# Sums of squares and a norm on TensorE, and two partial transforms in one PSUM bank, in a diffusion step's filter stage

## The chip, the cores and the metric

The kernel runs on one core of a Trainium2 chip. The metric is the time of one execution on the device, in microseconds (us). The engines are named as in the profile: TensorE is PE (its weight loads are PEld), VectorE is DVE, ScalarE is ACT, GpSimd is POOL, and SyncE (SP) issues DMAs.

## The reference

One inference step of a two-layer network on 1024 latent and 128 context tokens of width 1024: a layer of differential attention, then a Hyena layer with a long convolution, each followed by a SwiGLU layer. What the change touches is the first norm (`rmsnorm` ahead of the queries, keys and values) and the implicit filter of the convolution with its spectrum:

```python
def rmsnorm(x, g, eps=EPS):
    xf = x.astype(jnp.float32)
    y = xf * lax.rsqrt(jnp.mean(xf * xf, axis=-1, keepdims=True) + eps)
    return (y * g.astype(jnp.float32)).astype(x.dtype)

def implicit_filter(L, w1, b1, w2, b2, w3, b3, freq):
    ...
    h = (hdn @ w3.astype(f32) + b3.astype(f32)).reshape(L, 2, D_MODEL)
    ...
    h = h * jnp.exp(-t[:, None, None] * deltas)
    return h / (jnp.sum(jnp.abs(h), axis=(0, 1), keepdims=True) + FILT_EPS)

def bidir_fftconv(v, filt):
    ...
    kk = jnp.concatenate([h_f, jnp.zeros((1, D), filt.dtype), h_b[:0:-1]], axis=0)
    vf = jnp.fft.rfft(v.astype(jnp.float32), n=n, axis=1)
    kf = jnp.fft.rfft(kk, n=n, axis=0)
    return jnp.fft.irfft(vf * kf[None], n=n, axis=1)[:, :L]
```

## The kernel before

All data is float32, and large products are made of three TensorE matmuls on a high and a low part of each operand (`three`: high by high, low by high, high by low). A scheduler that simulates a timeline sets the order of each engine's instructions outside the stretches that the program pins; it takes buffers from pools as they come free. The pools that matter here: five PSUM banks `mm`, three PSUM banks `aux`, three buffers each of `wh`, `wl` and `bf`, two of `nsq`.

The first stage, `filters`, makes the filter and its spectrum for eight channel tiles of 128 channels, and beside it works off a generator, `start`, seven steps for each tile. `start` loads x, computes modulation vectors (`ada_step`, 32 small matmuls and a transpose each), and for each of three chunks of 384 tokens computes the row norm and the modulated input of the projection. Its norm: for each of eight row tiles, ScalarE squares x into `nsq`, GpSimd adds it into `nacc` (`square`, L445 and L449); then three one-column matmuls with a vector of ones sum `nacc` over partitions (L464), VectorE finishes the reciprocal root, and three matmuls with a diagonal (L484) broadcast it. Each of eight products and modulations follows (L553 to L557).

For a channel tile, `filter_time` computes the filter in time with 27 matmuls into five `mm` banks, VectorE multiplies by the decay into `filt` (L1425). ScalarE takes absolute values of the two combinations, VectorE their maximum (`am`), then sums it over eight blocks with stride 128 (L1442) and TensorE sums over partitions (L1447) for the norm `den`. GpSimd patches row 0 (L1453 to L1456). `hilo` splits each of two parts into high and low (L1432, L1433).

`filter_spectrum` transforms one part in four residues j = 0 to 3 of time modulo 4 (`dft`, six matmuls each). Residues 0 and 2 fill the two halves of one bank, 3 and 1 a bank each:

```python
        X3, X1 = self.mm(), self.mm()
        self.dft(X3, zh, zl, slice(0, 512), 3)
        self.dft(X1, zh, zl, slice(0, 512), 1)
        ...
        tt(f[:, 2], X1[:, part], s[:, part], ADD)
        tt(f[:, 3], X1[:, 1 - part], s[:, 1 - part], SUB)
```

ScalarE copies residue 3 to SBUF, VectorE makes the sum and difference (these butterflies have the line of the helper `tt`, L1288), GpSimd the last four, and a DMA stores them. Behind the stage come the projections `qk` (24 matmuls of 384 columns into each bank), which start with chunks 0 and 1 while chunk 2 is still being modulated.

## Time and profile before

| | |
|---|---|
| median of three runs | 3115.69 us (3109.5 to 3119.96) |
| the profiled execution | 3119.61 us, its span 3117.8 us |
| TensorE busy in the span | 3028.1 us (97%), weight loads 2957.7 us |
| VectorE, ScalarE, GpSimd busy | 1959.6, 1170.3, 964.1 us |
| mean granted TensorE clock | 0.990 of 2.4 GHz |

The span runs from the first instruction to the last; the rest of the execution's time, 1.8 us, lies outside it. Times of stretches are counted from the span's start. A matmul's record covers its way through the array, so records overlap, and a float32 matmul that is not split into parts leaves two records.

### The profile page before, as it was taken

The numbers are of one execution on the slowest core, as the hardware profiler recorded it, in microseconds if no ns is written. First come the engines' busy times: TensorE is split into PE (matmuls) and PEld (weight loads), VectorE is DVE, ScalarE is ACT, GpSimd is POOL, SyncE is SP. The second block draws the span as 40 slices with busy tenths as digits, with TensorE's granted clock in tenths as the row PEclk, the third lists the DMA queues.
The fourth block names the chain that finished last, engine by engine and source line by source line (L and its number), as shares of the span: only waits on it lengthen the run. The fifth ranks groups of instructions, "written<-read, shape, count | busy, mean of one in ns | idle before, by whom it ended". The sixth has DMA issues, their size and how long they took to land.

```text
span 3117.8 us, 52555 instructions
## 1 busy us (share of the span) xinstructions
PE 3028.1 (97%) x20963; PEld 2957.7 (95%) x20963; DVE 1959.6 (63%) x3223; ACT 1170.3 (38%) x2242; POOL 964.1 (31%) x842
## 2 busy tenths in 40 slices
PE   6889999999999999999999999999999999999998
PEld 5679999999999999999999999999999999999998
DVE  7866532888845745454568878876456444445555
ACT  3631123888835322223211442334644222222114
POOL 5844310444432334342000423221223343430003
PEclk9999999999999999999999999999999999999999
DMA  7665462334241222223555433345621222225211
GB/s 251 200 209 189 136 171 89 78 87 102 63 148 59 75 78 72 78 72 124 217 206 179 141 111 112 135 152 183 212 74 64 75 75 75 75 78 202 99 64 68
DMA packets 164635, 380.13 MB, mean 122 GB/s; under 512 B 17407, under 2 KB 80263, under 8 KB 161576
## 3 DMA queue, kind: packets, MB, share of 16 engines
q1 hardware_dynamic: 149016, 354.42, 34.6%
q10 hardware_dynamic: 13968, 17.65, 1.6%
q0 software_dynamic: 1408, 4.72, 0.4%
q8 instruction: 165, 2.70, 0.4%
q14 instruction: 78, 0.64, 0.1%
HBM read 279.99 MB, written 96.73 MB: 121 GB/s over the span
## 4 chain that ended last, share of the span: by engine, by line
PE 82%; DVE 5%; DMA 3%; issue 1%; POOL 1%; ACT 1%; SPq 0%; POOLq 0%; ACTq 0%; DVEq 0%
PE mm L308 12%; PE mm L310 12%; PE mm L309 12%; PE pr L310 11%; PE pr L308 11%; PE pr L309 10%; PE tr L820 4%; PE sc L794 2%; PE tr L811 2%; PE sc L795 2%; DMA araw<-ada_w 1%; DVE junk L402 1%; DVE xk L892 1%; DMA zt<-d_z 1%; DVE wl L1674 1%
## 5 line engine op out<-in xcount | busy, mean ns | idle before, releaser
L310 PE MATMUL mm<-hs,wl 128*128 128x384 f32 x1632 | 547.0, 336 | 0.0
L309 PE MATMUL mm<-hs,wh 128*128 128x384 f32 x1632 | 546.5, 335 | 0.4 <-POOL hs L498 0.3
L308 PE MATMUL mm<-hs,wh 128*128 128x384 f32 x1632 | 545.4, 336 | 0.9 <-DVE xk L892 0.9
L1288 DVE TENSOR_TENSOR xk<-pr,xk 128x576 f32<-128x576 f32 x202 | 152.5, 755 | 389.9 <-PE pr L310 203.9
L892 DVE SCALAR_TENSOR_TENSOR xk<-mm,ada,xk 128x192 f32<-128x192 f32 (+3 forms) x560 | 232.5, 453 | 255.4 <-PE mm L310 249.7
L449 POOL TENSOR_TENSOR nacc<-nacc,nsq 128x384 f32<-128x384 f32 x104 | 123.2, 1186 | 661.3 <-ACT nsq L445 659.3
L308 PEld LDWEIGHTS mm<-hs,wh 128*128 128x128 f32 x1632 | 306.2, 188 | 4.1 <-PE mm L310 1.5
L1673 ACT ACTIVATE wh<-raw 128x1024 fp32r<-128x1024 f32 x156 | 164.9, 1058 | 384.9 <-PE mm L309 333.8
L310 PEld LDWEIGHTS mm<-hs,wl 128*128 128x128 f32 x1632 | 306.4, 188 | 3.0 <-issue 1.6
L309 PEld LDWEIGHTS mm<-hs,wh 128*128 128x128 f32 x1632 | 306.4, 188 | 2.7 <-issue 0.6
L1288 POOL TENSOR_TENSOR xk<-xk,xk 128x576 f32<-128x576 f32 x80 | 116.8, 1461 | 524.9 <-DVE xk L1288 430.7
L1674 DVE TENSOR_TENSOR wl<-raw,wh 128x1024 fp32r<-128x1024 f32 x156 | 196.9, 1262 | 67.1 <-ACT wh L1673 66.7
L1674 DVE TENSOR_TENSOR wl<-xk,wh 128x512 fp32r<-128x512 f32 x160 | 174.1, 1128 | 48.3 <-ACT wh L1673 48.3
L308 PE MATMUL mm<-hh,wh 128*128 128x384 f32 x576 | 193.5, 339 | 2.4 <-ACT hh L556 1.8
L801 DVE TENSOR_REDUCE nm<-sc 128x1 f32<-128x1152 f32 x128 | 173.6, 1357 | 34.9 <-PE sc L795 34.8
L309 PE MATMUL mm<-hl,wh 128*128 128x384 f32 x576 | 194.6, 338 | 0.8 <-DVE hl L557 0.8
L310 PE MATMUL mm<-hh,wl 128*128 128x384 f32 x576 | 194.4, 338 | 0.0
L803 ACT ACTIVATE pr<-sc,nm 128x1152 f32<-128x1152 f32 x128 | 156.7, 1224 | 14.7 <-DVE nm L801 8.9
L1077 ACT ACTIVATE xk<-xk 128x576 f32<-128x576 f32 x40 | 27.4, 686 | 352.2 <-DVE xk L1288 352.2
L794 PE MATMUL sc<-kk,qs 128*128 128x384 f32 x384 | 140.5, 366 | 3.3 <-ACT pr L803 3.3
L820 PE MATMUL tr<-v,at 128*128 128x128 f32 x1152 | 139.4, 275 | 0.5 <-ACT at L815 0.5
L820 PEld LDWEIGHTS tr<-v,at 128*128 128x128 f32 x1152 | 133.8, 192 | 3.1 <-ACT at L815 0.9
(388 smaller groups left out, 8794.5 us busy)
## 6 DMA issues: line engine op xcount, KB each, us to landing
raw<-w_gu SPq DMA_DIRECT2D x88, 512.0 KB, 3.3
d_a<-xk SPq DMA_DIRECT2D x82, 288.0 KB
raw<-w_down SPq DMA_DIRECT2D x44, 512.0 KB, 4.2
araw<-d_a SPq DMA_DIRECT2D x36, 576.0 KB, 6.5
araw<-ada_w SPq DMA_DIRECT2D x36, 512.0 KB, 6.0
kk<-d_k SPq DMA_DIRECT2D x16, 1152.0 KB, 8.7
araw<-ada_t SPq DMA_DIRECT2D x28, 512.0 KB
raw<-w_in SPq DMA_DIRECT2D x24, 512.0 KB, 4.0
```

The costliest lines, as they stand in the source:

```text
L308: self.nc.tensor.matmul(out, ah, bh, start=first, stop=False, **kw)
L309: self.nc.tensor.matmul(out, ah, bl, start=False, stop=False, **kw)
L310: self.nc.tensor.matmul(out, al, bh, start=False, stop=last, **kw)
L449: nc.gpsimd.tensor_tensor(out=self.acc[c], in0=self.acc[c], in1=sq, op=ALU.add)
L794: nc.tensor.matmul(sc[:, c, :CH], lhs, kk[:, 0, p, ks], start=True, stop=False)
L801: nc.vector.tensor_reduce(out=nm, in_=sv, axis=AX.XY, op=ALU.max, negate=True)
L803: nc.scalar.activation(e.rearrange("p (a b) -> p a b", a=3), sv, AF.Exp, bias=nm, accum_out=st[hd][3][:, p, qt : qt + 1])
L820: self.nc.tensor.matmul(po[:, :P], at[:, b], v[:, b], start=b == 0, stop=b == 8)
L892: self.nc.vector.scalar_tensor_tensor(out=x, in0=ps[:, s:e], scalar=gate[:, d, g : g + 1], in1=x, op0=ALU.mult, op1=ALU.add)
L1288: (eng or self.nc.vector).tensor_tensor(out=o, in0=a, in1=b, op=op)
L1673: self.nc.scalar.activation(hi, x, AF.Copy)
L1674: (eng or self.nc.vector).tensor_tensor(out=lo, in0=x, in1=hi.bitcast(F32), op=ALU.subtract)
```

## The change

It does three things in the filter stage. The squares of `start` are no longer added by GpSimd: each is the stationary operand of three one-column matmuls with ones, which accumulate over the eight row tiles in one `aux` bank, and `rstd_parts` starts from that bank. The filter norm's sum over eight blocks is likewise done by eight accumulating one-column matmuls instead of VectorE's strided sum. And residues 1 and 3 accumulate in one bank: a second transform table (`k_filt`) holds residue 3 with the sine half negated, and for the second part the high and low parts of residue 3 are negated in `hilo`, so that the bank holds the sum in one half and the difference in the other.

```diff
--- before.py
+++ after.py
@@ -80,6 +80,9 @@
     ph = 2 * math.pi * ((2 * k[None, :] + 1) * tm[:, None] % 4096) / 4096
     fm = np.concatenate([np.cos(ph), -np.sin(ph)], axis=1)
     out["k_fwd"] = fm.reshape(2, P, 4, 512).transpose(1, 2, 0, 3).reshape(P, 8 * 512)
+    sign = np.ones((4, 512))
+    sign[3, 256:] = -1.0
+    out["k_filt"] = (fm.reshape(2, P, 4, 512) * sign).transpose(1, 2, 0, 3).reshape(P, 8 * 512)
     gm = fm.T / 1024.0
     out["k_inv"] = gm.reshape(4, P, 256, 4).transpose(1, 3, 0, 2).reshape(P, 16 * 256)
     k = np.arange(128)
@@ -458,8 +461,8 @@
 
     def rstd_parts(self, c, early=False):
         nc, acc = self.nc, self.acc[c] if isinstance(self.acc[c], tuple) else [self.acc[c]]
-        ps = self.aux()
-        for t in range(3):
+        ps = self.acc[c] if early else self.aux()
+        for t in range(0 if early else 3):
             for n, a in enumerate(acc):
                 nc.tensor.matmul(
                     ps[:, t : t + 1], a[:, P * t : P * t + P], self.ones[:, 0:1], start=n == 0, stop=n == len(acc) - 1
@@ -542,8 +545,19 @@
             return t
 
         for c in range(NCH):
+            self.acc[c] = self.aux()
             for k in range(KT):
-                self.square(c, k, source(c, k))
+                sq = self.tl(self.np_, [P, CH], tag="nsq", bufs=2)
+                nc.scalar.activation(sq, source(c, k), AF.Square)
+                for t in range(3):
+                    nc.tensor.matmul(
+                        self.acc[c][:, t : t + 1],
+                        sq[:, P * t : P * t + P],
+                        self.ones[:, 0:1],
+                        start=k == 0 and t == 0,
+                        stop=k == KT - 1,
+                        skip_group_check=True,
+                    )
                 yield
             rs = self.rstd(c, True)
             hh, hl = self.hpair()
@@ -1296,8 +1310,8 @@
             self.split(hi[:, o : o + step], lo[:, o : o + step], raw)
         return hi, lo
 
-    def forward_table(self, pool, raw_pool, raw_tag):
-        t = self.table(pool, self.i["k_fwd"], 4096, "t", raw_pool, raw_tag, 2048, 2 if raw_tag == "filt" else 1)
+    def forward_table(self, pool, raw_pool, raw_tag, src="k_fwd"):
+        t = self.table(pool, self.i[src], 4096, "t", raw_pool, raw_tag, 2048, 2 if raw_tag == "filt" else 1)
         self.fwd = [t.rearrange("p (j m f) -> p j m f", j=4, m=2) for t in t]
 
     def sine(self, halves, vec, j):
@@ -1360,7 +1374,7 @@
             c = slice(H * q, H * q + H)
             nc.scalar.activation(hids[0][:, c], hid[:, c], AF.Copy)
             nc.vector.tensor_tensor(out=hids[1][:, c], in0=hid[:, c], in1=hids[0][:, c].bitcast(F32), op=ALU.subtract)
-        self.forward_table(sp, sp, "filt")
+        self.forward_table(sp, sp, "filt", "k_filt")
         self.d_w = [self.tl(self.dp, [P, 2, P], F32, f"d_w{c}") for c in range(KT)]
         with self.tc.issue_after(mark.ins):
             w = [self.filter_weights(0), self.filter_weights(1)]
@@ -1387,10 +1401,10 @@
         for _ in rest:
             pass
 
-    def dft(self, out, zh, zl, cols, j):
+    def dft(self, out, zh, zl, cols, j, first=True, last=True):
         for m in range(2):
             a, f = 2 * j + m, [t[:, j, m, cols] for t in self.fwd]
-            self.three(out, zh[:, a], zl[:, a], *f, first=m == 0, last=m == 1)
+            self.three(out, zh[:, a], zl[:, a], *f, first=first and m == 0, last=last and m == 1)
 
     def filter_weights(self, ct):
         nc, i, sp, tt = self.nc, self.i, self.sp, self.tt
@@ -1423,14 +1437,21 @@
                 self.three(out, hid[0][:, t], hid[1][:, t], wh, wl)
             d = dec[:, a0 : a0 + m] if m == 2 else decp.unsqueeze(1)
             tt(filt[:, a0 : a0 + m], ps[:, : 256 * m].rearrange("p (a f c) -> p a f c", a=m, f=2), d.unsqueeze(2).to_broadcast([P, m, 2, P]), MUL)
-        sm = self.tl(sp, [P, 2, P], tag="fsum", bufs=1)
+        sm = self.tl(sp, [P, P], tag="fsum", bufs=1)
         self.zs = []
 
         def hilo(part):
             zh = self.tl(self.wp, [P, 8, P], F32R, tag="wh", bufs=3)
             zl = self.tl(self.wp, [P, 8, P], F32R, tag="wl", bufs=3)
-            nc.scalar.activation(zh, filt[:, 0:8, part], AF.Copy)
-            tt(zl, filt[:, 0:8, part], zh.bitcast(F32), SUB)
+            for a, b, sign in ((0, 6, 1.0), (6, 8, -1.0)) if part else ((0, 8, 1.0),):
+                z = filt[:, a:b, part]
+                nc.scalar.activation(zh[:, a:b], z, AF.Copy, scale=sign)
+                if sign > 0:
+                    tt(zl[:, a:b], z, zh[:, a:b].bitcast(F32), SUB)
+                else:
+                    nc.vector.scalar_tensor_tensor(
+                        out=zl[:, a:b], in0=z, scalar=sign, in1=zh[:, a:b].bitcast(F32), op0=MUL, op1=SUB
+                    )
             self.zs.append((zh, zl))
 
         am = self.tl(self.wp, [P, 8, P], tag="wh", bufs=3)
@@ -1439,12 +1460,12 @@
         nc.scalar.activation(am2, filt[:, 0:8, 1], AF.Abs)
         yield
         tt(am, am, am2, ALU.max)
-        nc.vector.tensor_reduce(out=sm[:, 0], in_=am.rearrange("p a c -> p c a"), axis=AX.X, op=ADD)
         nc.scalar.activation(am2[:, 0:2], filt[:, 8], AF.Abs)
-        tt(sm[:, 1], am2[:, 0], am2[:, 1], ALU.max)
+        tt(sm, am2[:, 0], am2[:, 1], ALU.max)
         ps = self.aux()
-        for g in range(2):
-            nc.tensor.matmul(ps[:, g : g + 1], sm[:, g], self.ones[:, 0:1], start=True, stop=True)
+        for a in range(8):
+            nc.tensor.matmul(ps[:, 0:1], am[:, a], self.ones[:, 0:1], start=a == 0, stop=a == 7)
+        nc.tensor.matmul(ps[:, 1:2], sm, self.ones[:, 0:1], start=True, stop=True)
         den = self.den[:, ct]
         nc.vector.tensor_scalar(out=den, in0=ps[:, 0:2], scalar1=FILT_EPS, scalar2=None, op0=ADD)
         nc.vector.reciprocal(den, den)
@@ -1468,22 +1489,19 @@
         X = self.mm()
         self.dft(X[:, 0:256], zh, zl, main, 0)
         self.dft(X[:, 256:512], zh, zl, main, 2)
-        s = self.tl(sp, [P, 2, 256], tag="xs", bufs=3)
-        nc.scalar.activation(s[:, 0], X[:, 256:512], AF.Copy)
-        tt(f[:, 0], X[:, 0:256], s[:, 0], ADD)
-        tt(f[:, 1], X[:, 0:256], s[:, 0], SUB)
-        X3, X1 = self.mm(), self.mm()
-        self.dft(X3, zh, zl, slice(0, 512), 3)
-        self.dft(X1, zh, zl, slice(0, 512), 1)
-        s = self.tl(sp, [P, 2, 256], tag="xs", bufs=3)
-        nc.scalar.activation(s, X3.rearrange("p (a b) -> p a b", a=2), AF.Copy)
-        X1 = X1.rearrange("p (a b) -> p a b", a=2)
-        tt(f[:, 2], X1[:, part], s[:, part], ADD)
-        tt(f[:, 3], X1[:, 1 - part], s[:, 1 - part], SUB)
-        tt(K[:, 0], f[:, 0], f[:, 2], ADD, nc.gpsimd)
-        tt(K[:, 2], f[:, 0], f[:, 2], SUB, nc.gpsimd)
-        tt(K[:, 1], f[:, 1], f[:, 3], SUB if part else ADD, nc.gpsimd)
-        tt(K[:, 3], f[:, 1], f[:, 3], ADD if part else SUB, nc.gpsimd)
+        s = self.tl(sp, [P, 256], tag="xs", bufs=3)
+        nc.scalar.activation(s, X[:, 256:512], AF.Copy)
+        tt(f[:, 0], X[:, 0:256], s, ADD)
+        tt(f[:, 1], X[:, 0:256], s, SUB)
+        Y = self.mm()
+        self.dft(Y, zh, zl, slice(0, 512), 1, last=False)
+        self.dft(Y, zh, zl, slice(0, 512), 3, first=False)
+        nc.scalar.activation(f[:, 2:4], Y.rearrange("p (a b) -> p a b", a=2), AF.Copy)
+        s, d = f[:, 2 + part], f[:, 3 - part]
+        tt(K[:, 0], f[:, 0], s, ADD, nc.gpsimd)
+        tt(K[:, 2], f[:, 0], s, SUB, nc.gpsimd)
+        tt(K[:, 1], f[:, 1], d, SUB if part else ADD, nc.gpsimd)
+        tt(K[:, 3], f[:, 1], d, ADD if part else SUB, nc.gpsimd)
         nc.scalar.dma_start(self.d_f[ct][:, part], K)
 
     def hyena_in(self, first):
```

What the scheduler made of it, in three places. The first is VectorE where the first channel tile's filter is finished, ahead of the first transform; `wh` and `wl` hold the maximum and the high and low parts, `th` and `tl` the table. Before:

```order
L1288 TENSOR_TENSOR filt_347<-mm_380,ndg_319 128x256
L1288 TENSOR_TENSOR wh_386<-wh_386,wl_387 128x1024
L1442 TENSOR_REDUCE fsum_385<-wh_386 128x128
L1288 TENSOR_TENSOR fsum_385<-wl_387 128x128
L1288 TENSOR_TENSOR wl_404<-filt_347,wh_403 128x1024
L1288 TENSOR_TENSOR wl_408<-filt_347,wh_407 128x1024
L1449 TENSOR_SCALAR den_218<-aux_394 128x2
L514 TENSOR_TENSOR tl_300<-filt_305,th_299 128x2048
```

Now:

```order
L1302 TENSOR_TENSOR filt_347<-mm_380,ndg_319 128x256
L1302 TENSOR_TENSOR wh_386<-wh_386,wl_387 128x1024
L1302 TENSOR_TENSOR fsum_385<-wl_387 128x128
L1302 TENSOR_TENSOR wl_410<-filt_347,wh_409 128x1024
L1302 TENSOR_TENSOR wl_414<-filt_347,wh_413 128x768
L1452 SCALAR_TENSOR_TENSOR wl_414<-filt_347,wh_413 128x256
L1470 TENSOR_SCALAR den_218<-aux_393 128x2
L1471 RECIPROCAL den_218<-den_218 128x2
L517 TENSOR_TENSOR tl_300<-filt_305,th_299 128x2048
```

The strided sum is gone, the second low part is two instructions, and what follows stands as it was.

The second is TensorE at the first row norm, between the filter products (`wsh`, `wsl`) of the third channel tile. Before and now:

```order
L382 MATMUL aux_582<-ident_203,ndg_580 128x128
L1447 MATMUL aux_697<-ones_207,fsum_646 128x1 x2
L464 MATMUL aux_771<-ones_207,nacc_587 128x1 x3
L309 MATMUL mm_834<-wsl_603,hidh_293 128x256
L310 MATMUL mm_834<-wsh_602,hidl_294 128x256
```

```order
L385 MATMUL aux_590<-ident_203,ndg_588 128x128
L553 MATMUL aux_595<-ones_207,nsq_596 128x1 x3
L553 MATMUL aux_595<-ones_207,nsq_601 128x1 x3
L1467 MATMUL aux_708<-ones_207,wh_663 128x1 x8
L1468 MATMUL aux_708<-ones_207,fsum_662 128x1
L553 MATMUL aux_595<-ones_207,nsq_606 128x1 x3
L311 MATMUL mm_884<-th_299,wh_724 128x256
```

In place of three sums of the finished `nacc` and two of the norm stand groups of three, one group for each square, and nine for the norm; of the chunk's eight groups three stand here and five between the transforms that follow.

The third is TensorE where the projection begins (`hh`, `hl` are its inputs, `aux` from `ndg` the broadcast of the third chunk's norm). Before, with the projection's products around it, and now, with those of the transform of the last tile but one:

```order
L309 MATMUL mm_2272<-hl_795,wh_2256 128x384
L310 MATMUL mm_2272<-hh_794,wl_2257 128x384
L308 MATMUL mm_2272<-hh_794,wh_2256 128x384
L309 MATMUL mm_2272<-hl_795,wh_2256 128x384
L484 MATMUL aux_1939<-ndg_1940,ones_207 128x128
L484 MATMUL aux_1939<-ndg_1943,ones_207 128x128
L1447 MATMUL aux_2075<-ones_207,fsum_2024 128x1 x2
L310 MATMUL mm_2272<-hh_794,wl_2257 128x384
L308 MATMUL mm_2272<-hh_794,wh_2256 128x384
```

```order
L313 MATMUL mm_2142<-th_299,wl_1961 128x256
L311 MATMUL mm_2142<-th_299,wh_1960 128x256
L487 MATMUL aux_1989<-ndg_1990,ones_207 128x128
L487 MATMUL aux_1989<-ndg_1993,ones_207 128x128
L1467 MATMUL aux_2120<-ones_207,wh_2075 128x1 x8
L1468 MATMUL aux_2120<-ones_207,fsum_2074 128x1
L312 MATMUL mm_2142<-tl_300,wh_1960 128x256
L313 MATMUL mm_2142<-th_299,wl_1961 128x256
L311 MATMUL mm_2159<-th_299,wh_1960 128x512
```

The broadcast and the last norm now stand ahead of the last transforms instead of inside the projection; the first projection product comes some 65 rows behind them. Past TensorE's row 1041 of 18124 the instructions are in the same order on all engines as before, apart from line and buffer numbers.

## Rows read from the trace of the kernel before

**Rows 1.** The page's slices: tenths busy of 40 slices of 78 us.
```profile
PE   6889999999999999999999999999999999999998
...
DVE  7866532888845745454568878876456444445555
```

**Rows 2.** Busy time by stretch: columns, the stage, three parts of it.
```profile
core 0: us, PE busy (x) PEld busy (x) DVE busy (x) ACT busy (x) POOL busy (x), PEclk, DMA share, GB/s
37.00:185.00 148.00, 128.40 (x1131) 108.48 (x1130) 128.68 (x202) 78.90 (x142) 106.75 (x123) 0.93 0.54 184
...
82.00:112.00 30.00, 23.32 (x234) 19.20 (x234) 25.46 (x38) 19.65 (x38) 25.96 (x32) 0.94 0.72 251
...
142.00:166.00 24.00, 20.43 (x188) 17.39 (x189) 21.22 (x31) 12.06 (x23) 14.95 (x18) 0.86 0.65 230
...
166.00:185.00 19.00, 19.00 (x118) 15.92 (x118) 15.24 (x28) 11.10 (x18) 10.84 (x12) 0.98 0.32 118
```

**Rows 3.** The waits of TensorE, 37 to 185 us: in total, times, longest.
```profile
PE mm L308 <- DVE filt L1288: 8.8, 3, 3.6
...
PE mm L310 <- DVE wl L1288: 3.2, 2, 2.9
...
PE mm L308 <- DVE bf L1288: 1.5, 1, 1.5
```

**Rows 4.** Groups by form, 37 to 185 us: busy and mean ns, idle before.
```profile
L449 POOL TENSOR_TENSOR nacc<-nacc,nsq 128x384 f32<-128x384 f32 x20 | 23.4, 1169 | 9.4 <-ACT nsq L445 8.9
...
L1288 DVE TENSOR_TENSOR bf<-mm,xs 128x256 f32<-128x256 f32 x60 | 22.1, 410 | 7.0 <-ACT xs L1479 3.1 <-PE mm L310 1.5 <-POOL nsq L1288 1.4
...
L1288 DVE TENSOR_TENSOR filt<-mm,raw 128x512 f32<-128x512 f32 x28 | 17.9, 678 | 0.4 <-PE mm L310 0.2
...
L1442 DVE TENSOR_REDUCE fsum<-wh 128x128 f32<-128x1024 f32 x8 | 16.3, 2039 | 0.1
```

**Rows 5.** The chain of waits, 172.5 to 175 us: start, us, what.
```profile
172.69 0.23 PE mm L310
...
173.04 0.34 PE aux L1447 x4
...
173.38 0.67 PE aux L464 x6
```

**Rows 6.** VectorE's timeline at the stage's start: start, us, operation, count, idle before.
```profile
35.33 2.00 DVE L1442 TENSOR_REDUCE fsum<-wh 128x128 f32<-128x1024 f32 x1
...
38.59 3.59 DVE L1288 TENSOR_TENSOR wl<-filt,wh 128x1024 fp32r<-128x1024 f32 x2 [0.64 <-ACT wh L1432]
```

**Rows 7.** TensorE's waits at the projection's start, 185 to 235 us.
```profile
PE aux L371 <- DMA araw<-ada_w: 2.0, 3, 1.3
...
PE mm L308 <- ACT hh L556: 1.8, 3, 1.0
...
PE mm L309 <- DVE hl L557: 0.8, 1, 0.8
```

**Rows 8.** Further waits, 37 to 185 us.
```profile
DVE wh L1288 <- ACT wl L1439: 6.6, 3, 3.8
...
POOL nsq L1288 <- DVE filt L1288: 4.1, 1, 4.1
...
ACT nsq L445 <- POOL nacc L449: 2.1, 4, 1.0
```

**Rows 9.** VectorE's timeline at three places.
```profile
81.60 3.79 DVE L553 TENSOR_TENSOR hl<-aux,hl 128x384 f32<-128x384 f32 x8
...
101.35 8.64 DVE L1288 TENSOR_TENSOR wl<-filt,wh 128x1024 fp32r<-128x1024 f32 x2 [0.68 <-ACT wh L1432]
...
161.59 1.21 DVE L1288 TENSOR_TENSOR wl<-filt,wh 128x1024 fp32r<-128x1024 f32 x1
```

**Rows 10.** TensorE's timeline behind two such blocks.
```profile
86.05 0.50 PE L308 MATMUL mm<-th,wh 128*128 128x512 f32 x1 [2.52 <-DVE filt L1288]
...
142.91 0.58 PE L308 MATMUL mm<-th,wh 128*128 128x256 f32 x1 [3.63 <-DVE filt L1288]
```

## The prediction

> **What bounds the kernel now.** The page's slices come first [rows 1]: TensorE is at nine tenths or more in all but the first few of 40 slices, each 78 us long. The reader should see that only slices 0 to 2 leave TensorE room, and that VectorE is fuller there than almost anywhere else. That is the filter stage, and every instruction the change touches lies in it or just behind it. The second view is busy time in that stage [rows 2]: from 37 us, where the first norm sum runs, to 185 us, where the query and key projection starts, VectorE works 128.7 of 148.0 us. TensorE's matmul records cover 128.4, its weight loads 108.5, GpSimd 106.8. So no engine is full, and VectorE is the tightest. TensorE's granted clock there is 0.93: (1 − 0.93) × 2 × 148 = 20.7 us at the lower of its two levels, 1.2 instead of 2.4 GHz, which costs half of that, 10.4 us. It is low where TensorE waits, 0.94 from 82 to 112 and 0.86 from 142 to 166 us, and 0.98 from there to 185, where its records leave no gap.
>
> The third view is who ended TensorE's waits [rows 3]: VectorE's filter products 8.8 us, its low parts 3.2, its butterflies 1.5, together 13.5. So in this stage TensorE runs behind VectorE, which is what the change unloads; but it loads TensorE.
>
> **Part by part.** All sums are against the profiled execution (span 3117.8, own time 3119.6 us); the median of the three runs, 3115.7, lies 3.9 lower.
>
> *Two partial transforms in one bank.* The matmul count stays: the four products of index 3 and index 1 go into one bank instead of two. VectorE loses two of four butterflies per part, 32 in all, at 410 ns [rows 4]: 13.1 us. ScalarE copies 512 columns as before, now into the result. The sign costs no instruction in part 0 (it is in the table, whose load has the same size) and splits the high and low part in part 1: eight more instructions on each of VectorE and ScalarE. VectorE's operations on 512 and 256 columns at 678 and 410 ns [rows 4] leave a fixed part of 0.142 us, so 1.1 us in eight; ScalarE works 78.9 of 148 us [rows 2] and hides its own.
>
> *The filter norm.* VectorE's eight strided sums of 2.04 us go, 16.3 us [rows 4]. TensorE gets nine one-column matmuls per channel tile instead of two: 56 more.
>
> *The sums of squares.* GpSimd's 21 additions go; 20 of them lie in the stage, 23.4 us [rows 4]. TensorE gets 72 one-column matmuls instead of 9: 63 more.
>
> *What the 119 cost.* Each float32 matmul appears as two records: in the chain, six records are three row-norm matmuls, 0.67 us, 0.112 us a record, and four records at the norm take 0.34 us [rows 5]. A 512-column matmul beside them takes 0.23, so a column count of one buys only half of it. 119 × 2 × 0.112 = **+26.6 us** of TensorE.
>
> Does TensorE have that room? By matmul records it is idle 19.6 of 148 us [rows 2], too little; by weight loads 39.5, enough. The added work is weight loads with almost nothing to stream, and I go by the loads. The Trainium skill ("Perfetto Trace Analysis", Identifying the Most-Contended Engine) says that matmul busy share is a poor measure of TensorE's headroom, since matmuls are pipelined, and to use that of weight loads. By it the added work fits; by the matmul records the stage would come out 7 us longer at least.
>
> *What TensorE gets back.* VectorE falls from 128.7 to 128.7 − 13.1 − 16.3 + 1.1 = 100.4 us, so the 13.5 us of waits for it can go: **−13.5** (0 to −13.5; the larger end, since 28 us is twice the wait). With TensorE denser the lower clock goes too: **−10.4** (0 to −10.4; the larger end, because it is 0.98 from 166 us, where TensorE does not wait).
>
> *The start of the stage.* In VectorE's timeline the first strided sum, 2.00 us, stands ahead of the low parts [rows 6], for which the first transform waits. It goes: **−2.0** (0, if ScalarE's copy, which already ends a wait of 0.64 there, is late; no more than 2.0).
>
> *The start of the projection.* As the order shows, the third token chunk's norm is broadcast before the last two transforms instead of inside the projection, so that chunk should be ready earlier. TensorE waits there 1.8 for its high parts and 0.8 for its low parts [rows 7]: **−2.6** (0 to −2.6). The waits for weights from DMA, 2.0, stay: SP's queue keeps its loads and only shifts the chunk's loads among them.
>
> *New waits.* A square's buffer, one of two, is freed by TensorE instead of GpSimd, and the row that patches the filter uses the same two; an auxiliary bank of three is held from a chunk's first square to its norm. Behind a late buffer stand ScalarE's next square and GpSimd's patch, and behind that the high parts and the transform. ScalarE waited 2.1 us for GpSimd there before, and GpSimd's patch 4.1 for VectorE [rows 8]. I take 0, the old wait for the new one; the ends are −2.1 and +4.1.
>
> Sum: 26.6 − 13.5 − 10.4 − 2.0 − 2.6 = **−1.9 us**: 3117.7 as profiled, 3113.8 on the scale of the median. Past the first projection tiles the instructions stand in the same order as before, so what the stage gains or loses is kept. A measurement of this kernel can tell about 0.3%, 9.3 us, from no change; this is within it.
>
> **Rivals.** *Faster.* The added loads fall into idle time that remains. Of the 39.5 us in which no weights load, 13.5 + 10.4 are used above; if the other 15.6 take part of the 26.6, only 11.0 lie on the path and the sum is −17.5 (3098.2 on the median's scale). For it: most added matmuls come in groups of three as each square is ready, scattered through the stage. VectorE may gain more than counted: two low-part operations took 8.64 us where GpSimd worked beside them, one took 1.21 us late in the stage, where GpSimd stood idle [rows 9]. The Trainium skill ("GPSIMD Engine Reference", Specifications) says that GpSimd and VectorE contend for SBUF when VectorE has two SBUF inputs; by that, less GpSimd work makes VectorE faster still, and the trace agrees (8.64 against 1.21). Against it: TensorE runs its queue in order, and a group waiting for a square holds up transforms behind it.
>
> *Slower.* TensorE becomes the bound while the waits stay. Two of the longest, 2.52 and 3.63 us, come behind blocks of eight norm products on VectorE, 3.79 us each, which the change does not touch [rows 9, 10]. If only the rest, 7.4, goes, and the clock stays low behind those two (0.94 over 30 us and 0.86 over 24 us, 1.8 + 3.4 lost [rows 2]), 5.2 comes back there and nothing at the two starts: 26.6 − 7.4 − 5.2 = +14.0, so 3129.7. It decides from where TensorE gets back less than 26.6 − 9.3 = 17.3 us of the 28.5 counted. Against it: VectorE has 28 us less ahead of these blocks.
>
> *The change does little to VectorE*, because its waits only move: VectorE ends as early but waits for ScalarE's absolute values (6.6 us before [rows 8]). Then the gains shrink by half, 26.6 − 14.2 = +12.4, so 3128.1; it counts with the slower case.
>
> **How the numbers follow.** No change 0.51, around 3113.8, on its own 3106 to 3125; faster 0.29, around 3098; slower 0.20, around 3129. The faster case gets more because one unknown, the overlap of scattered loads, works for it alone. The range, 3098 to 3127, takes in the faster case's middle and half of the slower one and leaves some 0.2 outside.
>
> **What would show it.** In the profile after: one-column matmuls at some 0.11 us a record, and TensorE's weight loads near 135 us in the stage; VectorE near 100 us; TensorE's waits for VectorE under 4 us; a granted clock over 0.97 between 64 and 166 us; the projection's first matmul within 5 us of 184. Wrong would be: the records far cheaper than 0.11 us; waits of TensorE for squares or for banks of some microseconds in all; a clock as low as before; or a time that moves without the stage moving.

## The result, and the profile after

The changed kernel takes 3135.55 us (median of 4, 3132.96 to 3136.44) where the kernel before, on the same chip, takes 3112.65 (4 runs): a ratio of 1.0064, 95% interval 1.0051 to 1.0077, some 20 us slower. That lies above the range given. The profiled execution after took 3135.16 us, its span 3133.4; the one before, at 3119.6, was 7 us slower than its median, so the two spans differ by 15.6 us and the medians by 22.9.

Busy time by stretch of the kernel after (PEclk is the granted clock), against [rows 2]:

```profile
core 0: us, PE busy (x) PEld busy (x) DVE busy (x) ACT busy (x) POOL busy (x), PEclk, DMA share, GB/s
37.00:185.00 148.00, 146.26 (x1228) 131.67 (x1229) 79.55 (x149) 73.34 (x136) 75.60 (x92) 0.83 0.49 168
...
166.00:185.00 19.00, 19.00 (x106) 16.66 (x101) 5.38 (x8) 5.77 (x10) 4.50 (x7) 0.50 0.43 131
...
37.00:211.30 174.30, 172.56 (x1370) 155.55 (x1371) 94.51 (x179) 84.74 (x158) 86.74 (x104) 0.82 0.46 157
```

All of TensorE's waits from 37 to 211 us (total, times, longest), against [rows 3]; then those of the projection's start, 211 to 262 us, against [rows 7]:

```profile
PE mm L311 <- ACT wh L1448: 0.9, 1, 0.9
PE mm L311 <- DVE filt L1302: 0.8, 1, 0.8
...
PE mm L311 <- ACT hh L570: 1.5, 1, 1.5
PE mm L312 <- DVE hl L571: 0.5, 1, 0.5
```

TensorE's timeline after: start, us, operation, count.

```profile
98.54 0.40 PE L312 MATMUL mm<-tl,wh 128*128 128x512 f32 x1
98.77 0.61 PE L487 MATMUL aux<-ndg,ones 128*128 128x128 f32 x4
99.22 1.84 PE L1467 MATMUL aux<-ones,wh 128*128 128x1 f32 x16
100.92 0.25 PE L1468 MATMUL aux<-ones,fsum 128*128 128x1 f32 x1
...
161.05 1.84 PE L1467 MATMUL aux<-ones,wh 128*128 128x1 f32 x16
162.75 0.36 PE L1468 MATMUL aux<-ones,fsum 128*128 128x1 f32 x2
162.98 1.48 PE L553 MATMUL aux<-ones,nsq 128*128 128x1 f32 x12
164.38 1.90 PE L374 MATMUL aux<-hl,cs 128*32 128x128 f32 x30
...
171.55 0.63 PE L311 MATMUL mm<-th,wh 128*128 128x512 f32 x1
171.98 0.63 PE L312 MATMUL mm<-tl,wh 128*128 128x512 f32 x1
...
185.98 3.41 PE L1467 MATMUL aux<-ones,wh 128*128 128x1 f32 x16
189.25 0.57 PE L1468 MATMUL aux<-ones,fsum 128*128 128x1 f32 x2
...
211.29 0.34 PE L311 MATMUL mm<-hh,wh 128*128 128x384 f32 x1
```

The reader should see three things. TensorE's waits, 13.5 us for VectorE alone before, are down to 1.7 in all: its records cover 146.26 of 148 us. VectorE fell from 128.7 to 79.6 us. And the clock, which was to rise, fell from 0.93 to 0.83, to 0.50 all the way from 166 to 185 us, where no record of TensorE leaves a gap. That drop begins behind 30 one-column records in a row (161.05 to 164.38), where the small matmuls of a modulation vector follow (L374). What it costs is in the same rows: 16 one-column records last 1.70 us at full clock (99.22 to 100.92) and 3.27 at the lower one (185.98 to 189.25), a transform's 512 columns 0.23 and 0.43. The projection starts at 211.3 us instead of 184.1.

So the time up to the projection splits as follows. The clock loses (1 − 0.82) × 174.3 = 31.4 us where it lost (1 − 0.93) × 147.1 = 10.3: **+21.1**. TensorE's idle time by records falls from 147.1 − 127.5 = 19.6 to 174.3 − 172.6 = 1.7: **−17.9**. The start moves by +27.2, so the added work comes to 27.2 − 21.1 + 17.9 = **+24.0**, near the 26.6 forecast. Behind the start 11.6 us comes back between the two profiles (27.2 against 15.6 in the spans), or 4.3 against the medians (22.9).

The column of the clock has a blind spot at the start: ahead of a trace's first clock record it reads 1.00. A product of 256 columns at 46 us, first in the kernel before, then after:

```profile
46.15 0.28 PE L310 MATMUL mm<-th,wl 128*128 128x256 f32 x1
```

```profile
46.08 0.41 PE L312 MATMUL mm<-tl,wh 128*128 128x256 f32 x1
```

TensorE came to its full clock (its warm-up) at 43.8 us before and at 48.4 after, by the first clock records; 0.93 and 0.83 count the time from 37 us to there as full. These 4.6 us more at the lower level cost 2.3, which belong to the clock and leave some 22 for the added work.

### The profile page after: what moved, and what is told of

It reads as the page before. It is cut to its first block, busy times and chain, and to the rows that moved or that the text cites. A ratio compares the mean times of both kernels' runs of the same rounds, so it can differ in the third digit from the quotient of the medians.

```text
span 3133.4 us, 52972 instructions
## 1 busy us (share of the span) xinstructions
PE 3067.5 (98%) x21201; PEld 3004.6 (96%) x21201; DVE 1919.4 (61%) x3191; ACT 1172.8 (37%) x2250; POOL 940.6 (30%) x821
## 4 chain that ended last, share of the span: by engine, by line
PE 88%; DMA 5%; DVE 3%; ACT 2%; issue 1%; POOL 1%; SPq 0%; ACTq 0%; POOLq 0%; DVEq 0%
PE mm L311 14%; PE mm L312 14%; PE mm L313 14%; PE pr L313 10%; PE pr L311 10%; PE pr L312 10%; PE tr L834 4%; PE sc L808 2%; PE sc L809 2%; PE tr L825 2%; DMA araw<-ada_w 1%; ACT xk L943 1%; PE aux L553 1%; PE tr L311 1%; PE tr L313 1%
## 5 line engine op out<-in xcount | busy, mean ns | idle before, releaser
L452 POOL TENSOR_TENSOR nacc<-nacc,nsq 128x384 f32<-128x384 f32 x83 | 98.2, 1184 | 649.3 <-ACT nsq L448 647.6
## 6 DMA issues: line engine op xcount, KB each, us to landing
kk<-d_k SPq DMA_DIRECT2D x16, 1152.0 KB, 11.6
```

Source lines behind the costliest of these rows:

```text
L452: nc.gpsimd.tensor_tensor(out=self.acc[c], in0=self.acc[c], in1=sq, op=ALU.add)
```

## The experiments

Two theories, in the words of the expectations. A: the one-column matmuls bring TensorE to its lower clock. B: any 26 us of added TensorE work costs this much on an engine that has become full. C, in the first runs: the new order of instructions is at fault. "Lower clock" is the time at the lower level from warm-up to the projection's first matmul, 2 × (1 − PEclk) × duration of that stretch, taken from the trace's clock records, which are finer than the two digits of the rows; each stretch's row stands with its run.

### The parts of the change alone

**The bank part alone** (`bank_only`): the change with its squares and its norm undone.

```diff
-                for t in range(3):
-                    nc.tensor.matmul(self.acc[c][:, t : t + 1], sq[:, P * t : P * t + P], self.ones[:, 0:1], ...)
+                self.square(c, k, source(c, k))
...
-        for a in range(8):
-            nc.tensor.matmul(ps[:, 0:1], am[:, a], self.ones[:, 0:1], start=a == 0, stop=a == 7)
+        nc.vector.tensor_reduce(out=sm[:, 0], in_=am.rearrange("p a c -> p c a"), axis=AX.X, op=ADD)
```

> Of the change only the two transforms in one bank; squares are added by GpSimd and the norm by VectorE's strided sum again. Theory A (the one-column matmuls bring TensorE's clock down): none are added, so the low clock stays at some 20 us or less in the stage, VectorE has 12 us less, and the time is 0 to 8 us below before. Theory B (any 26 us of added TensorE work costs this much): no work is added, also 0 to 8 us below. Theory C (the new order of the instructions is at fault): up to 10 us above before.

Measured: 3105.59 us against 3113.23 for the kernel before; ratio 0.9970 (0.9959 to 0.9982).

```profile
37.00:181.40 144.40, 127.77 (x1136) 109.72 (x1136) 118.37 (x186) 79.73 (x150) 105.26 (x121) 0.91 0.54 189
...
PE aux L374 <- DMA hl<-ada_w: 8.9, 4, 6.0
PE aux L487 <- DVE ndg L486: 3.3, 1, 3.3
```

The part is a gain of some 9 us. The waits for VectorE's products all but vanish, and a wait for weights from DMA, 8.9 us, takes their place.

**Bank and norm** (`norm_kept`): only the squares undone, the first half of the diff above.

> The change with the squares added by GpSimd again: one bank, and the filter norm on TensorE (56 one-column matmuls more, 12.5 us of TensorE at full clock). Theory A: low clock 25 to 40 us in the stage, in and behind the groups of eighteen records, 0 to 8 us above before. Theory B: 12.5 us of work against some 10 us of waits taken away, about as before, with the low clock at or under 20 us.

Measured: 3116.53; ratio 1.0003 (0.9993 to 1.0013). Lower clock 30.7 us.

```profile
37.00:189.90 152.90, 143.68 (x1248) 125.55 (x1247) 112.80 (x177) 80.63 (x152) 109.57 (x125) 0.90 0.51 178
```

**Bank and squares** (`squares_kept`): only the norm undone, the second half.

> The change with the norm's strided sum on VectorE again: one bank, and the squares on TensorE (63 one-column matmuls more, 14 us at full clock). Theory A: low clock 30 to 50 us, 5 to 12 us above before, the larger share of the loss because these groups lie scattered. Theory B: 14 us of work against waits taken away, 0 to 5 us above before, low clock at or under 20 us.

Measured: 3116.79; ratio 1.0005 (0.9996 to 1.0014). Lower clock 40.9 us.

```profile
37.00:192.60 155.60, 148.28 (x1259) 131.37 (x1260) 110.34 (x187) 82.41 (x154) 81.17 (x104) 0.87 0.50 176
```

Each costs 11 us over the bank part; both together cost 30. A new order of instructions (C) need not lose time, since the bank part has one and gains; it does not have the order of the whole change, so C stays open here.

**Streaming work instead** (`before_wide`): the kernel before with unused 512-column matmuls.

```diff
                 self.square(c, k, source(c, k))
+                self.dummy(hold, 3, k == 0)
...
         ps = self.aux()
+        self.dummy(ps, 7, True)
```

> The kernel before with 128 matmuls of 512 columns added that nothing reads (three behind each square, seven at each norm; 128 x 0.232 = 29.7 us of TensorE, more than the change adds), in a bank held as the change holds it. Theory A: these stream, so the low clock stays at 20 us or falls, and the time rises by 0 to 10 us. Theory B: the time rises by 20 us or more, as with the change.

Measured: 3128.95; ratio 1.0041 (1.0028 to 1.0054). Rows of two stretches:

```profile
19.00:54.00 35.00, 28.37 (x255) 24.16 (x259) 23.14 (x33) 14.61 (x28) 17.53 (x18) 0.51 0.91 346
54.00:199.30 145.30, 138.51 (x1050) 117.11 (x1039) 113.47 (x186) 72.46 (x129) 99.38 (x114) 0.95 0.44 154
```

The 0.51 at the start is no new loss: the kernel before runs at the lower level there too, unrecorded (products of 256 columns follow each other every 0.21 us up to 37 us, every 0.12 from 46 on). Its warm-up ends at 43.8 us, that of this profile at 53.3, which may be some 5 us of the 16. From there on the lower clock is 13.7 us against 20.5 before. So some 30 us of streaming work cost 16 us and did not lower the clock behind the warm-up, as A says; the time is above what A expected and below what B did. Work alone costs something (B), but less than the change did, though the change also freed VectorE.

### Streaming behind the one-column matmuls

**The changed kernel again** (`change_again`), no edit.

> The changed kernel once more, beside the three others of this group. Theory A (the one-column matmuls bring TensorE to its lower clock) and theory B (26.6 us of added TensorE work simply cost their length) both expect 3135, within 4 us. What differs is the clock from warm-up to the projection's first matmul: if the 61 us at the lower level belong to the kernel, there are again 50 us or more; if they were an accident of one profile, 35 or fewer, and A falls.

Measured: 3138.39; ratio 1.0065 (1.0050 to 1.0079). Lower clock 72 us.

```profile
37.00:213.20 176.20, 175.52 (x1369) 158.75 (x1369) 94.40 (x179) 84.72 (x157) 86.60 (x104) 0.80 0.45 155
```

**Streaming matmuls added to the change** (`after_wide`):

```diff
                 for t in range(3):
                     nc.tensor.matmul(...)
+                self.dummy(self.acc[c][:, P:], 2, False)
...
             nc.tensor.matmul(ps[:, 0:1], am[:, a], self.ones[:, 0:1], ...)
+            if a % 4 == 3:
+                self.dummy(ps[:, P:], 2, False)
```

> The changed kernel with unused streaming matmuls added (384 columns, rounded fp32): two behind each square's three one-column ones and two after each four of the norm's eight, 76 in all and some 13 us of TensorE work at full clock; the output is the same. Theory A: what follows a one-column group now streams, so the lower clock falls from 61 us to under 45, which gives back 8 us or more, and the time is within 6 us of the changed kernel's. Theory B: 13 us more work on an engine that is never idle in the stage, so the time is the changed kernel's plus 10 to 16, and the lower clock stays near 61 us.

Measured: 3151.72; ratio 1.0106 (1.0087 to 1.0124), 13 us over the change. Lower clock 37.5 us.

```profile
37.00:217.20 180.20, 176.73 (x1452) 158.18 (x1452) 97.91 (x181) 87.03 (x163) 82.19 (x103) 0.90 0.44 152
```

In the profile the clock did as A says; the time did as B says. But the profiled execution, 3141.56 us, is 10 us shorter than the median, and its mean clock over the whole span, 0.989, is not that of the other three, 0.985 to 0.986, which lie near the changed kernel's 0.983 to 0.985: inconclusive.

**Squares with the all-ones tile stationary** (`swapped_all`):

```diff
-                for t in range(3):
-                    nc.tensor.matmul(self.acc[c][:, t : t + 1], sq[:, P * t : P * t + P], self.ones[:, 0:1], ...)
+                nc.tensor.matmul(self.acc[c][:, :CH], self.ones, sq, start=k == 0, stop=k == KT - 1)
...
-            rs = self.rstd(c, True)
+            rs = self.rstd_wide(self.acc[c][:, :CH])
```

> The changed kernel with the squares summed the other way round: the all-ones tile is the stationary operand and the 384 squares stream, one matmul of two records for a square where there were three of two, and the sum stands in every partition, so that the norm is computed on 384 columns by VectorE (5 operations of 0.3 to 0.5 us for a chunk, an estimate from its 384-column rows) and the diagonals with their 9 matmuls go. At 0.11 us for a record of 128 such columns, a record of 384 takes 0.32, and 24 squares 15.4 us, against 72 x 2 x 0.112 = 16.1 us of the change: the same work, but streaming. Theory A: the lower clock falls from 61 us to 45 or fewer (the norm's one-column matmuls stay), and the time falls by 6 us or more from the changed kernel, to 3129 or less. Theory B: equal work, equal time, within 4 us of the changed kernel.

Measured: 3126.42; ratio 1.0033 (1.0021 to 1.0045). Lower clock 34 us.

```profile
37.00:205.80 168.80, 156.98 (x1255) 131.90 (x1255) 110.58 (x169) 85.50 (x157) 85.52 (x103) 0.90 0.46 159
```

**The same with the norm left on VectorE** (`swapped_bank`): the norm's half of the first diff as well.

> The bank part of the change and the squares summed with the all-ones tile stationary, the norm's strided sum left on VectorE: against the run with the squares as the change has them (3116.8, lower clock 40.9 us before the projection) the TensorE work is the same, but nearly no one-column matmul is left in the stage. Theory A: the lower clock is 27 us or fewer, as with the bank part alone, and the time 3111 or less. Theory B: 3116.8, within 4 us. If TensorE now waits for VectorE's longer norm, its waits there are over 2 us a chunk and the time may be up to 6 us above either.

Measured: 3121.43; ratio 1.0015 (1.0004 to 1.0027). Lower clock 13.7 us against 40.9 with one column.

```profile
37.00:189.40 152.40, 134.67 (x1126) 107.12 (x1126) 114.45 (x168) 80.92 (x148) 80.73 (x100) 0.96 0.50 172
...
93.52 0.81 PE L564 MATMUL aux<-nsq,ones 128*128 128x384 f32 x2
93.86 0.58 PE L311 MATMUL mm<-wsh,hidh 65*128 65x256 f32 x1
...
PE mm L311 <- DVE filt L1306: 6.0, 2, 5.7
PE mm L311 <- DVE bf L1306: 5.3, 1, 5.3
```

The clock rose in both as A says. The time does not separate the theories, for two reasons. A square's two records take 0.34 us (93.52 to 93.86), not the 0.64 of the expectation, so the work was not equal. And VectorE, which now has the norm on 384 columns, kept TensorE waiting 11.3 us.

### The same instructions with 128 columns

The test that alters least: every added one-column matmul writes 128 equal columns, of which one is read. The instructions are the same, but the scheduler sets their order anew.

**All of them** (`wide128_all`):

```diff
-                        self.acc[c][:, t : t + 1],
+                        self.acc[c][:, P * t : P * t + P],
                         sq[:, P * t : P * t + P],
-                        self.ones[:, 0:1],
+                        self.ones,
...
-            nc.tensor.matmul(ps[:, 0:1], am[:, a], self.ones[:, 0:1], start=a == 0, stop=a == 7)
-        nc.tensor.matmul(ps[:, 1:2], sm, self.ones[:, 0:1], start=True, stop=True)
+            nc.tensor.matmul(ps[:, 0:P], am[:, a], self.ones, start=a == 0, stop=a == 7)
+        nc.tensor.matmul(ps[:, P : 2 * P], sm, self.ones, start=True, stop=True)
```

> The changed kernel with each of its added one-column matmuls writing 128 equal columns: the same stationary blocks in the same order, with 128 columns of the all-ones tile streamed behind each instead of 1, and one of the 128 read. At full clock a record of 128 such columns took 0.11 us, as one of a single column did, so TensorE has the same number of matmuls and loads and the same work. Theory A (what brings the clock down is that almost nothing streams behind these loads): from warm-up to the projection's first matmul the lower clock falls from 61 and 72 us to 40 or fewer, and the time falls by 10 us or more from the changed kernel's 3135 to 3138. Theory B (loads on a full TensorE cost their length, and the clock follows something else): lower clock 55 us or more, time within 4 us of the changed kernel's, or up to 10 above if 128 columns do add to a record.

Measured: 3118.51; ratio 1.0009 (1.0000 to 1.0018), so 17 to 20 us less than the changed kernel. The page's busy times and instruction counts, the changed kernel's first; then of the widened one two stretches, TensorE's timeline and its longest waits up to the projection:

```profile
PE 3067.5 (98%) x21201; PEld 3004.6 (96%) x21201; DVE 1919.4 (61%) x3191; ACT 1172.8 (37%) x2250; POOL 940.6 (30%) x821
```

```profile
PE 3039.9 (98%) x21201; PEld 2976.3 (96%) x21201; DVE 1926.0 (62%) x3191; ACT 1172.2 (38%) x2250; POOL 944.4 (30%) x821
...
37.00:186.00 149.00, 144.11 (x1371) 129.07 (x1371) 96.84 (x177) 82.37 (x155) 83.55 (x102) 0.99 0.53 183
...
146.00:162.00 16.00, 16.00 (x160) 13.95 (x159) 4.25 (x11) 5.47 (x11) 5.71 (x8) 1.00 0.67 216
...
89.07 1.95 PE L1468 MATMUL aux<-ones,wh 128*128 128x128 f32 x16
90.86 0.39 PE L1469 MATMUL aux<-ones,fsum 128*128 128x128 f32 x2
...
148.77 1.95 PE L1468 MATMUL aux<-ones,wh 128*128 128x128 f32 x16
...
150.78 1.50 PE L554 MATMUL aux<-ones,nsq 128*128 128x128 f32 x12
...
152.33 1.07 PE L374 MATMUL aux<-hl,cs 128*32 128x128 f32 x28
...
185.97 0.34 PE L311 MATMUL mm<-hh,wh 128*128 128x384 f32 x1
...
PE mm L311 <- ACT wh L1449: 1.8, 1, 1.8
PE mm L311 <- DVE filt L1303: 1.5, 2, 0.8
PE mm L313 <- DVE wl L1303: 1.2, 1, 1.2
```

The counts are equal on every engine, 16 records last 1.79 us against 1.70, the clock goes from 0.82 to 0.99 and the projection starts at 186.0 instead of 211.3. This is not one lucky profile: the mean clock over the whole span is 0.983 to 0.985 in all nine executions of the changed kernel and 0.992 to 0.994 in all eleven of this one. TensorE idles more than in the change (4.9 against 1.7 us).

The order is not held equal, but the place where the changed kernel loses its clock for longest stands here too: 16, 2 and 12 added records in a row, with a modulation vector's small matmuls behind them, from 148.77 here (one product stands between) and from 161.05 there. Here the clock stays at 1.00. A holds: it is how little streams behind these weight loads that brings the clock down, not the loads, their count or a gap, and at this place not their order.

**Norm or squares alone** (`wide128_norm`, `wide128_squares`): the matching half of that diff, on the kernels with one part kept.

> The bank part and the norm's part of the change, the squares left on GpSimd, and the norm's one-column matmuls widened to 128 equal columns. Beside it stands the run with one column: 3116.5, 30.7 us at the lower clock before the projection. Theory A: 20 us or fewer at the lower clock, and a time 4 to 8 us lower, 3109 to 3112; the norm's 12.5 us of loads still cost something over the bank part alone (3105.6). Theory B: 3116.5, within 4 us.

Measured: 3113.27; ratio 0.9993 (0.9983 to 1.0003).

```profile
37.00:183.00 146.00, 132.64 (x1247) 116.48 (x1246) 100.47 (x177) 79.47 (x149) 111.87 (x126) 0.98 0.55 187
```

> The bank part and the squares' part of the change, the norm's strided sum left on VectorE, and the squares' one-column matmuls widened to 128 equal columns. Beside it stands the run with one column: 3116.8, 40.9 us at the lower clock before the projection. Theory A: 27 us or fewer, as with the bank part alone, and 3108 to 3112. Theory B: 3116.8, within 4 us.

Measured: 3116.20; ratio 1.0005 (0.9996 to 1.0014).

```profile
37.00:190.30 153.30, 139.37 (x1257) 120.43 (x1258) 108.64 (x180) 81.05 (x151) 83.61 (x105) 0.97 0.51 177
```

The clock rose in both, to 0.98 and 0.97, yet the times fell by only 3.3 and 0.6 us. Where TensorE is not yet the only bound, a faster TensorE waits instead: its idle time by records grew from 152.9 − 143.7 = 9.2 to 13.4 and from 7.3 to 13.9 us. The clock's full price is paid where nothing else is late, as in the whole change.

**VectorE's sum as a tree** (`bank_tree`): the bank part, and no TensorE work for the norm.

```diff
-        nc.vector.tensor_reduce(out=sm[:, 0], in_=am.rearrange("p a c -> p c a"), axis=AX.X, op=ADD)
+        tt(am[:, 0:4], am[:, 0:4], am[:, 4:8], ADD)
+        tt(am[:, 0:2], am[:, 0:2], am[:, 2:4], ADD)
+        tt(sm[:, 0], am[:, 0], am[:, 1], ADD)
```

> The bank part of the change alone (3105.6 in its own run), with VectorE's strided sum over the norm's eight blocks replaced by three contiguous additions of 512, 256 and 128 columns; TensorE gets no work. A strided sum took 2.0 us and more, the three additions should take 1.2 to 1.5 by the 512- and 256-column rows of VectorE. Theory A and theory B both hold that VectorE's relief is worth little where it is paid with TensorE's time; here it is not paid at all. In the bank part's trace TensorE waits for VectorE some 7 us in the stage and 8.9 for weights from DMA, so I expect 3102 to 3106; 3098 or less would say that VectorE's strided sum does bound the stage.

Measured: 3116.90; ratio 1.0004 (0.9995 to 1.0013). VectorE's groups of its three additions:

```profile
L1291 DVE TENSOR_TENSOR wh<-wh 128x512 f32<-128x512 f32 x7 | 8.1, 1159 | 0.1
...
L1291 DVE TENSOR_TENSOR wh<-wh 128x256 f32<-128x256 f32 x8 | 6.1, 768 | 0.0
L1291 DVE TENSOR_TENSOR fsum<-wh 128x128 f32<-128x128 f32 x8 | 4.6, 574 | 0.2
```

A miss: the three take 1.16 + 0.77 + 0.57 = 2.5 us, more than the strided sum's 2.04 [rows 4]. The rows they were sized by [rows 4] read one operand from PSUM; these read both from SBUF. The maximum beside them (`fsum` from `wl`) takes longer as well, 1.62 us against 0.51 in the bank part, and VectorE works 127.6 us up to the projection instead of 118.4. Why the maximum does is open.

### Was the old low clock the same thing?

**The kernel before and the bank part, their own one-column matmuls widened** (`before_w128`, `bank_w128`; 23 ahead of the projection in the one, 25 in the other), and **the bank part once more** (`bank_again`, no edit).

```diff
-                    ps[:, t : t + 1], a[:, P * t : P * t + P], self.ones[:, 0:1], ...
+                    ps[:, w * t : w * t + w], a[:, P * t : P * t + P], self.ones[:, 0:w], ...
...
-            nc.tensor.matmul(ps[:, g : g + 1], sm[:, g], self.ones[:, 0:1], start=True, stop=True)
+            nc.tensor.matmul(ps[:, P * g : P * g + P], sm[:, g], self.ones, start=True, stop=True)
```

> The kernel before with the one-column matmuls it had already in this stretch (two for each filter group's norm, three for each token chunk's) widened to 128 equal columns; nothing else moves. Theory A, carried over: they are part of why the kernel before ran 20.5 us at the lower clock between warm-up and the projection. Then there are 10 us or fewer, and the time is 2 to 6 us lower, 3108 to 3112. Rival: the 23 matmuls are too few, and the lower clock there comes from TensorE's waits for VectorE (2.5 to 3.6 us each). Then 17 us or more stay, and the time within 2 us.

Measured: 3115.40; ratio 1.0001 (0.9991 to 1.0012).

```profile
37.00:185.00 148.00, 129.17 (x1126) 110.41 (x1125) 118.16 (x195) 77.45 (x139) 110.01 (x125) 0.91 0.53 182
```

> The bank part of the change alone, with the same 23 one-column matmuls widened to 128 equal columns. Theory A, carried over: of its 27.3 us at the lower clock before the projection 13 or fewer are left, and the time is 2 to 7 us under the bank part's own. Rival (waits bring the clock down there): 20 us or more stay, and the time within 2 us of the bank part's.

Measured: 3111.72; ratio 0.9991 (0.9982 to 1.0000).

```profile
37.00:181.60 144.60, 125.74 (x1127) 106.47 (x1127) 121.28 (x175) 78.54 (x148) 104.31 (x125) 0.92 0.53 185
```

> The bank part of the change alone, once more, beside the two others: 3105.6 in its first run. If its gain is real, 3103 to 3109; if that run was lucky, 3110 to 3115, as near to the kernel before as the bank part with the tree of additions came.

Measured: 3105.37; ratio 0.9970 (0.9957 to 0.9983): the bank part's gain is real, and it is the fastest version of this study, faster than both kernels.

Widening left the clock about where it was, 0.91 and 0.92 against 0.93 and 0.91. So the few one-column matmuls of the kernel before are not the whole cause of its low clock. They may have a part: where the kernel before falls to the lower level right behind ten of their records, at 64 us, the widened one stays at the full one up to 78 us, and falls elsewhere instead. TensorE's waits remain the likely cause of the rest, as the prediction had it, but no run took them away alone. Why the widened bank part is 6 us slower than the bank part stays open; its profile has a wait of 5.0 us for VectorE and one of 4.0 for ScalarE that the other lacks.

## Why the prediction was wrong

**The step that failed** is "With TensorE denser the lower clock goes too: −10.4". The clock's loss went from 10.3 to 31.4 us instead: +21.1 where −10.4 stood, 31 us of error in a sum that missed by 25 (−1.9 against +22.9). I had read from [rows 2] that the clock is low where TensorE waits and full where it does not, and took the density of records as the cause. A row of the kernel before that these rows pass over speaks against it:

```profile
64.00:82.00 18.00, 18.00 (x105) 16.82 (x105) 17.53 (x34) 7.59 (x12) 10.38 (x15) 0.81 0.37 124
```

TensorE's records leave no gap in these 18 us, and the clock is the lowest of any part of the stage. Ahead of the stretch stand a wait of 0.98 us and ten one-column records (63.34 to 64.48). The added records are dense in time and stream one column each; the widened kernel shows that this is what counts. It has the clock the forecast asked for, 0.99, and its ratio is 1.0009 (1.0000 to 1.0018), 0 to 6 us over the kernel before. So with its clock as assumed the time lies in the forecast's range. Of the prediction's signs of being wrong this one occurred, "a clock as low as before", and none of the other three: a record took 0.106 us, no wait for a square or a bank is left, and the time moved with the stage.

The Trainium skill ("TensorE: Matmul & The Clock Gate", Why this matters for your kernels) ties a drop of the clock in mid-kernel to idle gaps between bursts of matmuls. By it the clock should have risen here. The trace of this case differs: 0.50 from 166 to 185 us without a gap, and the widened kernel had more idle time and 0.99. The measurement decides.

**+26.6 of work** was near: 24.0 by the split above, 22 with the later warm-up. In the widened kernel the start moves by 186.0 − 184.1 = 1.9 us, the clock's loss by 1.5 − 10.3 = −8.8 and the idle time by 4.9 − 19.6 = −14.7, which gives 25.4, or 28 with its warm-up, which ends at 38.8 us, 5.0 earlier than before.

**"By it the added work fits"** misled less, but it misled. Loads left 39.5 us idle; the work still cost its length less only the idle time by matmul records that went, 17.9 us. The Trainium skill ("Perfetto Trace Analysis", Identifying the Most-Contended Engine) prefers the loads as the measure of room. Here the runs side with the matmul records: even in the widened kernel loads cover only 129.07 of 149 us, and it is no faster than before.

**Waits for VectorE, −13.5,** went, and some others with them. VectorE fell further than forecast, to 79.6 instead of 100.4 us in the stage, mostly because the stage's last instructions now lie beyond 185 us: up to the projection it works 94.5.

**The new waits (0)** were right: no wait for a square or an auxiliary bank is left. **The stage's start (−2.0)** came in part: the first transform starts at 44.45 us instead of 45.45. **The projection's start (−2.6)** had the sign and the size by luck. The waits that the term named are still there, 1.5 us for the high parts and 0.5 for the low ones where they were 1.8 and 0.8 [rows 7]; what went are the wait for weights from DMA, 2.0, which the prediction kept, and one of 1.5 for a diagonal.

**The rivals.** The slower one had the sign (+14.0) but a mechanism that did not occur: it kept the waits. The faster one failed with the clock; its sum had also counted the clock's 10.4 among the 39.5 us in which no weights load, though a load at the lower clock is not idle time. What would have been needed is a fourth one: the waits go, and the clock falls because of what is added.

## What to carry to other kernels

A one-column matmul on TensorE cost as much here as one of 128 columns, and many of them on a full TensorE can cost the clock as well: a 512-column product behind them took 0.43 us instead of 0.23. If such sums must be on TensorE, widen the streamed side to 128 equal columns: here it cost 0.1 us in 16 records and gave back 17 to 20 us. Moving work from VectorE to TensorE paid here only up to the idle time in TensorE's matmul records, so try a change's parts one by one: one of three gained and the other two each took that gain back.

## What the hardware showed that was not expected

- The granted clock fell to 0.50 while TensorE's records left no gap, with one-column matmuls in the stretch, and stayed at 0.99 with the same matmuls at 128 columns.
- 16 float32 records of a 128 x 128 stationary operand last 1.70 us with 1 column and 1.79 with 128 at full clock, and 3.27 with 1 column at the lower level.
- The lower clock can also last without one-column matmuls and without a gap: behind a wait of 12.7 us the kernel before runs filter products of 65 rows and 256 columns from 25 to 37 us, one every 0.21 us, as at the lower level, and comes to the full clock only at 43.8. From 166 to 185 us in the changed kernel such products take some 6 us and one-column records another 6; so what keeps the clock low there need not be the latter alone.
- On VectorE one strided sum of 1024 to 128 columns (2.04 us) took less than three contiguous additions of 512, 256 and 128 (2.5 us).
